# Two encoder layers on one core: three more couples of the down-projections by seven products, weight sums in place, split pieces through a ring of six

## The chip, the core and the metric

The kernel runs on one core of a Trainium2 chip. The core has a matrix engine (TensorE, PE in the profile; the loading of its stationary operand is listed as PEld), VectorE (DVE), ScalarE (ACT), GpSimd (POOL) and SyncE (SP), which here only issues DMAs, and 16 DMA engines that move data between HBM and the on-chip memory. Engines run their own instruction streams and wait for one another by semaphores. The metric is the device time of one execution in microseconds, as the median of several runs.

## The reference

What must be computed is a two-layer encoder trunk over 256 tokens of width 2048, in float32. Layer 0 mixes tokens by a bidirectional mLSTM, layer 1 by a bidirectional HGRN2. Each mixer and each feed-forward block has an RMSNorm ahead and a residual sum behind, and a last RMSNorm closes the trunk. The change is in the feed-forward blocks (and in what they share with the mixers' output projections):

```python
def conv_glu(hn, w_up, conv_w, conv_b, w_down):     # D_FF = 5504, CONV_W = 3
    u = hn @ w_up
    a, v = jnp.split(u, 2, axis=-1)
    s = a.shape[1]
    pad = CONV_W // 2
    ap = jnp.pad(a, ((0, 0), (pad, pad), (0, 0)))
    c = conv_b
    for j in range(CONV_W):
        c = c + ap[:, j:j + s] * conv_w[j]
    return (jax.nn.gelu(c, approximate=False) * v) @ w_down
...
for layer in range(DEPTH):
    hn = rmsnorm(h, norm_mix_g[layer])
    h = h + (mlstm_mixer if layer == 0 else hgrn_mixer)(hn, ...)
    h = h + conv_glu(rmsnorm(h, norm_ffn_g[layer]), ...)
return rmsnorm(h, final_g)
```

## The kernel before, in words

**Split products.** A float32 product is made of matmuls in a reduced format: each operand is a high part plus the rest, and high x high, high x rest and rest x high are summed. `parts` makes the two pieces of a weight: ScalarE copies a loaded tile to the high part `wh` (L137), VectorE subtracts it to get `wl` (L138). Both have four buffers of 1024 columns (`WB`). A weight tile arrives in one of three `raw` buffers by a DMA that SP issues.

**The stream.** All weight-heavy work is one list of chunks that `stream` runs through in order, with `split_weights` fetching pieces three ahead (`LOOK`). There are three kinds. An "fm" chunk holds 16 k-tiles and gives 256 features by 256 tokens with the weights stationary (L328 and L332). A "tm" chunk gives 256 tokens by 512 features with the activations stationary (L344). An "st" chunk, made by `pair`, gives two blocks of 512 output features at once by 2x2 squares of Strassen and Winograd: two k-tiles form a couple, in which the activations are A11, A12, A21, A22 (two token halves by two k-tiles) and the weights B11, B12, B21, B22. A plain couple takes eight products of three matmuls (128 x 512), a couple "by seven" takes seven of them, with four sums of activations (S1 to S4, `token_sums`) and four sums of weights (T1 to T4, `weight_sums`) in place of the plain operands. Products are accumulated in eight PSUM banks: four `mm` banks for P1, P5, P6 and P7 and four `aux` banks named `pc` for C11 to C22 (L237). After the last couple by seven, `mid` adds the four P banks to the residual `hm` in the on-chip memory (L546 to L554; the last two adds are on POOL), and after the last couple of the chunk `done` adds the four C banks (L559).

**A feed-forward block.** It has two parts, with 22 and 21 of the 43 blocks of 128 features. Part 0 is 22 fm chunks for the up-projection, then two pairs over the same 22 k-tiles, d0 and d1, 11 couples each. Part 1 is 21 fm chunks, one pair d0 of ten couples and a single k-tile, and then two tm chunks for the rest of the output, d2. Behind each fm chunk `done_up` scales by the norm's R, makes the convolution (a middle tap with the bias, then two shifted taps), Gelu, the product by v and the split of the result, which becomes the stationary operand of the pair. `SEVEN` says which couples go by seven: 7 of 11 in d0 of part 0, 6 in d1, and 6 in the pair of part 1, so 19 in each layer.

**Where weight sums come from.** For six couples of each pair (`STORED`) the sums are worked out beforehand: during the fm chunks `prepare` loads the four squares of a couple into four tiles (tags `th0`, `th1`, `tl0`, `tl1`), runs `weight_sums` on VectorE, and writes the sums to a scratch in HBM (`tscr`). In the pair, `combine` gets them back as two tiles `T` of 1024 columns and splits them into `th0`, `tl0`, `th1`, `tl1` (L209 and L210), each with one buffer. The seventh couple of d0 has its sums made on the spot. The outer projections of the mixers use the same code through `mixed`, with three couples by seven of eight (`SEVEN_MIX`), their sums made on the spot.

**What sets the order.** Each engine's instruction stream is put in order at build time by a scheduler that simulates the program; only instructions given to `pin` are kept where they are written. Extra work on the side (`prepare`, late norms) is a generator that `side.tick` advances as the matmuls are emitted. SP issues its DMAs in its own order, the loads for weights and for sums together with the stores of sums. TensorE's code itself is brought in by a DMA queue, listed in the profile as an instruction queue. In the HGRN mixer, which lies between the two feed-forward blocks, every head has a burst of many tiny float32 matmuls (`pd` and `pa`, L984), and the heads come in four groups.

Of the kernel before, what the change touches and what calls it, by code (L numbers as in the profile page):

```python
# [15 lines left out]
P = 128  # L16
# [27 lines left out]
WB = 4  # L44
MIX = 5
# [3 lines left out]
SEVEN = (1, 2, 4, 5, 7, 8, 9), (1, 2, 4, 5, 7, 8), (1, 2, 4, 5, 7, 8)  # L49
STORED = (1, 2, 4, 5, 7, 8)  # L50
# [10 lines left out]
def trunk_kernel(ctx, tc, xT, x_d, fg_d, pp_d, cst_d, w_gate, w_first, w_aq, w_ak, w_av, w_ao, w_aout, w_ao2,  # L61
# [63 lines left out]
    pin = tc.keep_in_program_order  # L125

# [5 lines left out]
    def split_weights(chunks):  # L132

        def parts(r, m, pin=lambda ins: ins):
            wh = wpool.tile([P, 1024], F32R, tag="wh", bufs=WB, name="wh")
            wl = wpool.tile([P, 1024], F32R, tag="wl", bufs=WB, name="wl")
            pin(act.copy(wh[:, :m], r))  # L137
            pin(dve.tensor_tensor(wl[:, :m], r, wh[:, :m].bitcast(F32), ALU.subtract))  # L138
            return wh, wl
# [33 lines left out]
    def temporary(pool_, name):  # L173
        return pool_.tile([P, 1024], F32, tag="avc", bufs=TEMP if pool_.name == "ff" else 2, name=name)

    def weight_sums(a, b, T, T_):

        B22, B21, B12 = a[:, 512:1024], b[:, 0:512], b[:, 512:1024]
        dve.tensor_tensor(T.rearrange("p (a b) -> p a b", a=2), B12.unsqueeze(1).broadcast_to([P, 2, 512]),
                          a.rearrange("p (a b) -> p a b", a=2), ALU.subtract)  # L180
        yield 2.5
        dve.tensor_tensor(T_[:, 0:512], B22, T[:, 0:512], ALU.subtract)
        yield 2.5
        dve.tensor_tensor(T_[:, 512:1024], B21, T_[:, 0:512], ALU.subtract)

    def split_squares(ch, parts):

        units, raws, kept, sums = (ch.nk + 1) // 2, {}, {}, {}
        side.until(lambda: ch.waits is None or ch.waits)

        def raw(u):
            if u not in raws and u < units:
                raws[u] = load_raw(ch.src, 2048 * u, min(2048 * (u + 1), 1024 * ch.nk) - (512 if u in ch.stored else 0))
                if u in ch.stored:
                    kept[u] = [temporary(ch.pool, "T") for _ in range(2)]
                    for t, src in zip(kept[u], ch.stored[u]):
                        nc.sync.dma_start(t, src)
            return raws.get(u)

        def combine(u):  # L200
            r = raw(u)
            T, T_ = kept[u] if u in kept else (temporary(ch.pool, "T") for _ in range(2))
            if u not in kept:
                for _ in weight_sums(r[:, 0:1024], r[:, 1024:2048], T, T_):
                    pass
            sums[u] = []
            for i, t in enumerate((T, T_)):
# [1080 lines left out]
```

## Time and profile before

| what | value |
|---|---|
| median of 3 runs | 2391.03 us (2389.68 to 2392.11) |
| span of the profiled execution | 2388.5 us, 2.5 us less than that median |
| TensorE busy | 2372.4 us, 99% of the span, at full clock |
| VectorE busy | 1944.1 us, 81% |
| ScalarE busy | 1298.8 us, 54% |
| POOL busy | 189.7 us, 8% |
| DMA | 555.07 MB, mean 232 GB/s |

The profile is one execution of the program, taken on the core; its times are microseconds from the start of the span. The page gives each engine's busy time, the chain of work that ended last (from the last instruction back, at each step to what released it), the costliest groups of instructions and the DMAs. A row of a group reads: line, engine, operation, output <- input by the program's names, shape and count, then busy time, mean nanoseconds of one, and the idle time just before them with what ended it. A row of a chain or a timeline reads: start, duration, engine, line, and what it is. A row of the windows reads: start and end, then the sum of the busy times of the engines in the order that the text gives, with numbers of instructions, then the granted clock, the DMA engines' busy share, and GB/s.

### The profile page before, as it was taken

The numbers are of one execution on the slowest core, as the hardware profiler recorded it, in microseconds if no ns is written. First come the engines' busy times: TensorE is split into PE (matmuls) and PEld (weight loads), VectorE is DVE, ScalarE is ACT, GpSimd is POOL, SyncE is SP. The second block draws the span as 40 slices with busy tenths as digits, with TensorE's granted clock in tenths as the row PEclk, the third lists the DMA queues.
The fourth block names the chain that finished last, engine by engine and source line by source line (L and its number), as shares of the span: only waits on it lengthen the run. The fifth ranks groups of instructions, "written<-read, shape, count | busy, mean of one in ns | idle before, by whom it ended". The sixth has DMA issues, their size and how long they took to land.

```text
span 2388.5 us, 37988 instructions
## 1 busy us (share of the span) xinstructions
PE 2372.4 (99%) x14614; PEld 2030.4 (85%) x14614; DVE 1944.1 (81%) x3221; ACT 1298.8 (54%) x2013; POOL 189.7 (8%) x240
## 2 busy tenths in 40 slices
PE   9999999999999999999999999999999999999998
PEld 7888888888888888888888888888888888888887
DVE  7766687988887888777888888888889888788874
ACT  7655455454564554555555555555555565454563
POOL 0100000000000000001222222220000000000000
PEclk9999999999999999999999999999999999999999
DMA  8654556988787777755554554545798888677774
GB/s 300 201 180 165 183 178 211 333 294 317 269 293 254 251 239 262 273 194 182 173 171 168 175 177 160 177 166 188 258 325 298 298 281 296 231 249 263 249 266 148
DMA packets 98789, 555.07 MB, mean 232 GB/s; under 512 B 11168, under 2 KB 11680, under 8 KB 50736
## 3 DMA queue, kind: packets, MB, share of 16 engines
q1 hardware_dynamic: 96912, 548.64, 65.6%
q0 software_dynamic: 1120, 3.21, 0.7%
q8 instruction: 114, 1.87, 0.3%
q10 hardware_dynamic: 576, 0.79, 0.1%
q14 instruction: 67, 0.55, 0.1%
HBM read 512.69 MB, written 39.91 MB: 231 GB/s over the span
## 4 chain that ended last, share of the span: by engine, by line
PE 98%; DVE 1%; issue 1%; DMA 0%; ACT 0%; SPq 0%; POOLq 0%; POOL 0%
PE mm L328 37%; PE mm L344 23%; PE mm L332 18%; PE pc L237 12%; PE mm L237 5%; PE pn L776 1%; PE py L1034 1%; PE pd L984 1%; PE pz L405 0%; PE pa L984 0%; DMA raw<-in_w_first 0%; PE S L762 0%; DVE tl L210 0%; PE pz L1055 0%; PE pa L1009 0%
## 5 line engine op out<-in xcount | busy, mean ns | idle before, releaser
L328 PE MATMUL mm<-xt,wh 128*128 128x512 f32 x3776 | 1313.4, 394 | 0.0
L137 ACT CAST wh<-raw 128x1024 fp32r<-128x1024 f32 (+1 forms) x846 | 853.5, 1019 | 693.8 <-PE mm L328 237.9
L138 DVE TENSOR_TENSOR wl<-raw,wh 128x1024 fp32r<-128x1024 f32 (+1 forms) x846 | 1004.7, 1195 | 265.1 <-ACT wh L137 257.6
L332 PE MATMUL mm<-xt,wl 128*128 128x256 f32 x3776 | 1045.9, 278 | 0.0
L328 PEld LDWEIGHTS mm<-xt,wh 128*128 128x128 f32 x3776 | 706.2, 188 | 159.4
L332 PEld LDWEIGHTS mm<-xt,wl 128*128 128x128 f32 x3776 | 709.5, 188 | 4.5 <-issue 0.4
L344 PE MATMUL mm<-wh,xt 128*128 128x512 f32 x1024 | 320.5, 391 | 3.0 <-ACT xt L350 1.3
L344 PEld LDWEIGHTS mm<-wh,xt 128*128 128x128 f32 x1024 | 191.4, 188 | 43.3 <-ACT xt L350 1.7
L344 PE MATMUL mm<-wl,xt 128*128 128x512 f32 x512 | 198.2, 391 | 0.0
L237 PE MATMUL pc<-wh,g 128*128 128x512 f32 x508 | 167.2, 389 | 0.0
L355 ACT COPY b<-mm 128x256 f32<-128x256 f32 x236 | 87.4, 370 | 122.9 <-PE mm L332 122.7
L210 DVE TENSOR_TENSOR tl<-T,th 128x1024 fp32r<-128x1024 f32 x88 | 109.9, 1264 | 38.9 <-ACT th L209 36.7
L209 ACT CAST th<-T 128x1024 fp32r<-128x1024 f32 x88 | 92.7, 1054 | 73.6 <-PE mm L237 43.5
L237 PEld LDWEIGHTS pc<-wh,g 128*128 128x128 f32 x508 | 95.4, 188 | 19.9
L344 PEld LDWEIGHTS mm<-wl,xt 128*128 128x128 f32 x512 | 96.2, 188 | 18.9
L553 POOL TENSOR_TENSOR hm<-hm,u 128x512 f32<-128x512 f32 x8 | 10.4, 1302 | 1150.9 <-DVE u L552 1150.9
L237 PE MATMUL pc<-wl,g 128*128 128x512 f32 x254 | 98.9, 389 | 0.0
L344 PE MATMUL mm<-wh,g 128*128 128x512 f32 x308 | 96.6, 392 | 0.0
L237 PE MATMUL mm<-th,sx 128*128 128x512 f32 x264 | 91.9, 390 | 0.0
L356 DVE TENSOR_TENSOR avc<-mm,b 128x256 f32<-128x256 f32 x172 | 72.0, 418 | 14.7 <-ACT b L355 14.7
L361 DVE TENSOR_TENSOR avc<-avc,R 128x256 f32<-128x256 f32 x172 | 71.9, 419 | 1.6
L976 DVE COPY kq<-QK 128x256 f32<-128x256 f32 x224 | 69.7, 336 | 0.0
(260 smaller groups left out, 2476.7 us busy)
## 6 DMA issues: line engine op xcount, KB each, us to landing
raw<-in_w_up SPq DMA_DIRECT2D x172, 1024.0 KB, 5.5
raw<-in_w_d SPq DMA_DIRECT2D x48, 1024.0 KB, 5.0
raw<-in_w_bq SPq DMA_DIRECT2D x48, 1024.0 KB, 4.9
pth<-in_w_d SPq DMA_DIRECT2D x72, 512.0 KB, 6.7
tscr<-ptl SPq DMA_DIRECT2D x72, 512.0 KB, 4.7
T<-tscr SPq DMA_DIRECT2D x72, 512.0 KB, 5.1
raw<-in_w_d SPq DMA_DIRECT2D x36, 768.0 KB, 5.2
raw<-in_w_ao SPq DMA_DIRECT2D x24, 1024.0 KB, 4.8
```

Source lines behind the costliest of these rows:

```text
L137: pin(act.copy(wh[:, :m], r))
L138: pin(dve.tensor_tensor(wl[:, :m], r, wh[:, :m].bitcast(F32), ALU.subtract))
L209: act.copy(th, t)
L210: dve.tensor_tensor(tl, t, th.bitcast(F32), ALU.subtract)
L237: pe.matmul(ps, a, b, start=id(ps) not in begun, stop=stop and i == 2)
L328: pe.matmul(ps[f], wh[:, c:c + P], x, start=k + kk == 0, stop=False)
L332: pe.matmul(ps[f][:, 0:T], wl[:, c:c + P], x[:, 0:T], start=False, stop=k + kk == ch.nk - 1)
L344: pe.matmul(ps[t], x[:, a + t * P:a + (t + 1) * P], w[:, c], start=st and i == 0, stop=sp and i == 2)
L355: act.copy(b, ps[:, T:2 * T])
L356: dve.tensor_tensor(dst, ps[:, 0:T], b, ALU.add)
L361: dve.tensor_tensor(dst, dst, R, ALU.mult)
L976: dve.tensor_copy(m[:, j].rearrange("k (m p j) -> k m p j", p=2, j=h), blocks(z, h, 0, T))
```

## The change

- `SEVEN` becomes 8 couples of 11 in both pairs of part 0 and 6 of 10 in part 1: 22 couples by seven in each layer. All of them have their sums stored, and `STORED` is gone. The scratch holds 2 x 8 + 6 sets of sums for each layer instead of 18.
- `prepare` loads a couple's four squares into two tiles of 1024, one couple ahead, computes the four sums in place with four subtractions of 512 columns, and stores both tiles. Their tags are `wh` and `wl` of the feed-forward pool, with two buffers each (`MORE`).
- In an st chunk the split pieces all go through `parts`. Every third one takes the feed-forward pool's two buffers, so that `wh` and `wl` have six in all. A couple by seven has four pieces, in the order B11 and B22, T2 and T3, B21 and T1, T4, and the matmuls follow it. Pieces are fetched three ahead, as before, and each of the four counts as one. T1 is loaded into the free last quarter of the `raw` tile, the rest of the sums into one tile `T` of 1536 columns. `th` and `tl` are gone.
- In `done_up` the conv's middle tap is made by ScalarE (an activation with scale and bias) instead of VectorE, and the two products by R become one of 512 columns. The bounce tile `b` is left out there.
- `token_sums` writes S4 to the unused half of the last-but-one activation tile or to a tile of its own.
- `banks` allocates the `mm` banks two at a time, by the same tag as before.

```diff
-SEVEN = (1, 2, 4, 5, 7, 8, 9), (1, 2, 4, 5, 7, 8), (1, 2, 4, 5, 7, 8)
-STORED = (1, 2, 4, 5, 7, 8)
+MORE = 2
+SEVEN = (1, 2, 3, 4, 6, 7, 8, 9), (1, 2, 4, 5, 7, 8)
...
-        def parts(r, m, pin=lambda ins: ins):
-            wh = wpool.tile([P, 1024], F32R, tag="wh", bufs=WB, name="wh")
-            wl = wpool.tile([P, 1024], F32R, tag="wl", bufs=WB, name="wl")
+        def parts(r, m, pin=lambda ins: ins, more=None):
+            where, bufs = wpool, WB
+            if more is not None:
+                turns["w"] += 1
+                if turns["w"] % 3 == 0:
+                    where, bufs = more, MORE
+            wh, wl = (where.tile([P, 1024], F32R, tag=n, bufs=bufs, name=n) for n in ("wh", "wl"))
             pin(act.copy(wh[:, :m], r))
             pin(dve.tensor_tensor(wl[:, :m], r, wh[:, :m].bitcast(F32), ALU.subtract))
             return wh, wl
...
         def raw(u):
             if u not in raws and u < units:
-                raws[u] = load_raw(ch.src, 2048 * u, min(2048 * (u + 1), 1024 * ch.nk) - (512 if u in ch.stored else 0))
+                n = 1536 if u in ch.stored else min(2048, 1024 * ch.nk - 2048 * u)
+                raws[u] = load_raw(ch.src, 2048 * u, 2048 * u + n)
                 if u in ch.stored:
-                    kept[u] = [temporary(ch.pool, "T") for _ in range(2)]
-                    for t, src in zip(kept[u], ch.stored[u]):
-                        nc.sync.dma_start(t, src)
+                    kept[u] = temporary(ch.pool, "T")
+                    nc.sync.dma_start(kept[u], ch.stored[u][:, 0:1536])
+                    nc.sync.dma_start(raws[u][:, 1536:2048], ch.stored[u][:, 1536:2048])
             return raws.get(u)
...
         for u in range(units):
             r = raw(u)
-            if u + 1 in ch.seven and not ch.late:
+            yield *parts(r[:, 0:1024], 1024, more=ch.pool), 1
+            if u + 1 in ch.seven and u + 1 not in ch.stored:
                 combine(u + 1)
...
+            if u in ch.seven:
+                yield *parts(kept[u][:, 0:1024], 1024, more=ch.pool), 1
             if 2 * u + 1 < ch.nk:
...
+                yield *parts(r[:, 1024:2048], 1024, more=ch.pool), 1
+            if u in ch.seven:
+                yield *parts(kept[u][:, 1024:1536], 512, more=ch.pool), 1
...
             if u in ch.seven:
...
+                S1, S3, S2, S4 = ch.sums(u)
+                products((P1, A11, B11), (C12, S4, B22))
+                T2, T3 = piece()
+                products((P6, S2, T2), (P7, S3, T3))
+                B21, T1 = piece()
+                products((C11, A12, B21), (P5, S1, T1))
+                T4, _ = piece()
+                products((C21, A22, T4))
...
     def prepare(mp, todo, period, finished):
...
+        yield 18.0
+        load(0)
+        for i, (_, dst) in enumerate(todo):
+            yield period / 2
+            load(i + 1)
+            B11, B22, B21, B12 = (loaded[i][j // 2][:, j % 2 * 512:(j % 2 + 1) * 512] for j in range(4))
+            for x, y, out in ((B12, B22, B22), (B12, B11, B12), (B11, B22, B11), (B21, B11, B21)):
+                dve.tensor_tensor(out, x, y, ALU.subtract)
+                yield period / 8
+            for j in range(2):
+                nc.sync.dma_start(dst[:, j * 1024:(j + 1) * 1024], loaded[i][j])
...
-                fm_scaled(ps[0], R, a)
-                fm_scaled(ps[1], R, v)
+                for z, p in ((a, ps[0]), (v, ps[1])):
+                    act.copy(z, p[:, T:2 * T])
+                    dve.tensor_tensor(z, p[:, 0:T], z, ALU.add)
+                av = avc[:, 0:2 * T].rearrange("p (a b) -> p a b", a=2)
+                dve.tensor_tensor(av, av, R.unsqueeze(1).broadcast_to([P, 2, T]), ALU.mult)
                 cw = [col("conv_w", (layer * 3 + w) * FT + f) for w in range(3)]
-                dve.tensor_scalar(c, a, cw[1], col("conv_b", layer * FT + f), ALU.mult, ALU.add)
+                act.activation(c, a, AF.Identity, bias=col("conv_b", layer * FT + f), scale=cw[1])
```

More of the change, by code (lines that the diff above doesn't have):

```diff
@@ L198, in raw @@
             return raws.get(u)
         def combine(u):
[L201 to L207, printed above, removed]
[L208 to L211 removed]
+            r, T = raw(u), temporary(ch.pool, "T")
@@ L594, in sums @@
             return SX[u]
-        two = pair(w2, KT, 1, x, sums, norm, SEVEN_MIX, True)
+        two = pair(w2, KT, 1, x, sums, norm, SEVEN_MIX)
         def token():
@@ L1152, in two @@
                 return ch
-            chunks.append(two(w_d0[layer][:, f0 * 1024:(f0 + nf) * 1024], 0, nxt if part else None, SEVEN[2 * part]))
+            chunks.append(two(w_d0[layer][:, f0 * 1024:(f0 + nf) * 1024], 0, nxt if part else None, SEVEN[part]))
             if part:
@@ L1159, in ffn @@
             else:
-                chunks.append(two(w_d1[layer], 2, None, SEVEN[1]))
+                chunks.append(two(w_d1[layer], 2, None, SEVEN[0]))
         return chunks, stack.close
```

128 lines of the change are left out of this document (62 added, 66 removed).

## The prediction, made before the result was known

> **What bounds the kernel now.** I read the page first, then the waits of TensorE, then a table by stage.
>
> ```profile
> span 2388.5 us, 37988 instructions
> PE 2372.4 (99%) x14614; PEld 2030.4 (85%) x14614; DVE 1944.1 (81%) x3221; ACT 1298.8 (54%) x2013; POOL 189.7 (8%) x240
> ...
> PE 98%; DVE 1%; issue 1%; DMA 0%; ACT 0%; SPq 0%; POOLq 0%; POOL 0%
> ```
>
> TensorE is busy all the time and is 98% of the chain that ends last. So time goes only with TensorE's own instructions or with its few waits, and it comes only from a new wait of TensorE. These are its waits (in all, times, longest):
>
> ```profile
> PE pd L984 <- issue: 2.6, 2, 1.4
> ...
> PE mm L344 <- issue: 0.9, 1, 0.9
> PE mm L344 <- ACT wh L137: 0.8, 1, 0.8
> PE mm L237 <- DVE tl L210: 0.6, 2, 0.3
> ```
>
> In layer 0 the stages that the change touches are the first up-projections (22 chunks), the pair d0, the pair d1, the other 21 up-projections, and the last pair. The columns are busy time of PE, PEld, DVE, ACT, POOL, then clock, DMA share and GB/s:
>
> ```profile
> 389.70:635.30 245.60, 245.60 (x1421) 214.78 (x1420) 215.77 (x363) 128.45 (x192) 0.70 (x1) 1.00 0.82 295
> 635.30:690.40 55.10, 55.10 (x245) 45.63 (x244) 44.20 (x51) 33.88 (x40) 0.00 (x0) 1.00 0.84 296
> 690.40:747.00 56.60, 56.30 (x248) 46.09 (x247) 46.99 (x48) 31.56 (x35) 7.09 (x4) 1.00 0.74 262
> 747.00:979.90 232.90, 232.90 (x1344) 203.64 (x1344) 194.01 (x317) 117.81 (x174) 0.00 (x0) 1.00 0.73 250
> ```
>
> Full clock, no gap in PE but 0.3 us, VectorE and the DMA engines at four fifths: this is what a new wait has to come from.
>
> **The change part by part.** *Three more couples by seven products in each layer (19 to 22).* A product is three matmuls of 128x512, so 6 couples take away 18 matmuls. The chain shows a whole plain couple:
>
> ```profile
> 1027.79 5.44 PE pc L237 x24
> ```
>
> 5.44 / 24 = 0.2267 us each; 18 x 0.2267 = 4.1 us less. Nothing lies beside TensorE, so all of it counts: **-4.1 us**.
>
> *TensorE's code moves.* Waits put down to "issue" stand in three of the four groups of heads of the HGRN layer, always at the end of a head's burst of tiny matmuls. The chain has them:
>
> ```profile
> 1206.43 0.70 PE pd L984 x41
> 1207.13 1.24 issue
> 1208.37 0.26 PE pd L984 x5
> ```
>
> ```profile
> 1330.86 0.71 PE pd L984 x42
> 1331.56 1.38 issue
> ```
>
> ```profile
> 1455.39 0.73 PE pd L984 x43
> 1456.13 0.66 PE mm L344 x2
> 1456.79 0.87 issue
> ```
>
> And the fourth group, as a window, has none (PE 1.60 of 1.60):
>
> ```profile
> 1579.00:1580.60 1.60, 1.60 (x130) 1.56 (x130) 1.57 (x4) 1.48 (x5) 0.00 (x0) 1.00 0.04 10
> ```
>
> The code comes by a queue of its own:
>
> ```profile
> q8 instruction: 114, 1.87, 0.3%
> ```
>
> 29228 records of PE and PEld in 114 packets are 256 instructions a packet. A head's burst (line 984) is 64 float32 matmuls of four instructions each: one block, gone in 1.3 us. If a block's edge lies at the start of the burst, the next edge lies at its end, before the next block can be there. I counted TensorE's instructions in the built order (two for a split matmul or a transpose, four for a plain float32 one, one for a wait). All three stalls are at the same place, count 195 modulo 256, and the four bursts begin 9 after, 2 after, 5 before and 12 before that edge. So the position decides: 1.24, 1.38, 0.87 and 0 us. In the changed kernel everything from here on lies 16 earlier (9 matmuls less in layer 0, two waits more). The four bursts then begin 7, 14, 21 and 28 before the edge; in the other twelve the edge lies 62 to 216 instructions inside, as now (46 to 200). Between 5 and 12 before, 0.87 falls to 0, so 7 before gives about 0.6. The waits' 2.6 + 0.9 = 3.5 us become 0.6: **-2.9 us**; the ends are -3.5 (all gone) and 0 (as many as now). I take the first reading, since one position fits all four rows.
>
> [...]
>
> *Splits through a ring of six; the sums' own single buffers go.* TensorE's 0.6 us behind `tl` arose when d1 follows d0. There POOL adds to hm, and a VectorE instruction stands still beside it:
>
> ```profile
> 693.31 0.68 DVE L552 TENSOR_TENSOR u<-u,mm 128x512 f32<-128x512 f32 x1
> 693.90 0.68 DVE L559 TENSOR_TENSOR hm<-hm,pc 128x512 f32<-128x512 f32 x1
> 694.50 4.27 DVE L210 TENSOR_TENSOR tl<-T,th 128x1024 fp32r<-128x1024 f32 x2
> ```
>
> ```profile
> 695.41 2.29 POOL L554 TENSOR_TENSOR hm<-hm,u 128x512 f32<-128x512 f32 x1
> ```
>
> ```profile
> 682.40 2.35 DVE L138 TENSOR_TENSOR wl<-raw,wh 128x1024 fp32r<-128x1024 f32 x2
> ...
> 684.67 2.35 DVE L210 TENSOR_TENSOR tl<-T,th 128x1024 fp32r<-128x1024 f32 x2
> ```
>
> The same two splits take 4.27 instead of 2.35 us: 1.9 us lost. With six pieces ahead instead of a single `tl` this loss is covered there: **-0.6 us** (ends -0.6 and 0). But the built order of layer 0 puts VectorE's work so: after P5 is complete four adds of mid, two splits for d1, and only then the add that frees the bank of C11, which d1's first matmul needs. By the starts above an add takes 0.6 us and a split 1.14: 4 x 0.6 + 2 x 1.14 + 0.6 = 5.3, and 7.2 with POOL's 1.9. TensorE has 27 matmuls left, 6.1 us. So a new wait of **+1.1 us** (0 if POOL falls elsewhere). In layer 1 the built order has the bank's add ahead of POOL's work: 0.
>
> *VectorE and ScalarE in the up stages.* These are the durations:
>
> ```profile
> L138 DVE TENSOR_TENSOR wl<-raw,wh 128x1024 fp32r<-128x1024 f32 x782 | 963.8, 1237 | 257.0 <-ACT wh L137 249.6
> L210 DVE TENSOR_TENSOR tl<-T,th 128x1024 fp32r<-128x1024 f32 x88 | 109.9, 1264 | 38.9 <-ACT th L209 36.7
> L361 DVE TENSOR_TENSOR avc<-avc,R 128x256 f32<-128x256 f32 x172 | 71.9, 419 | 1.6
> L179 DVE TENSOR_TENSOR ptl<-pth 128x1024 f32<-128x1024 f32 x36 | 44.0, 1223 | 26.5 <-DMA pth<-in_w_d 22.7 <-issue 3.6
> L138 DVE TENSOR_TENSOR wl<-raw,wh 128x512 fp32r<-128x512 f32 x64 | 43.9, 686 | 8.1 <-ACT wh L137 8.1
> L1118 DVE TENSOR_SCALAR avc<-avc,pp 128x256 f32<-128x256 f32 x86 | 34.9, 406 | 0.0
> L532 DVE TENSOR_TENSOR avc<-avc 128x128 f32<-128x128 f32 x104 | 30.0, 288 | 2.0
> L182 DVE TENSOR_TENSOR ptl<-pth,ptl 128x512 f32<-128x512 f32 x36 | 24.6, 683 | 0.0
> ```
>
> In the first up stage the middle tap leaves VectorE (22 x 0.41 = -8.9), two multiplications by R become one of 512 (22 x (2 x 0.42 - 0.68) = -3.5), 16 preparations of 4 x 0.68 stand for 12 of 1.22 + 2 x 0.68 (+12.6), and token sums are 8 instead of 7 with one instruction more (+3). That is +3 on 215.8 of 245.6 us: hidden, 27 us of room. ScalarE gets 22 taps of about the Gelu's length, +9 on 128. If VectorE waited for each tap, the room allows 1.2 us a chunk before TensorE is touched. The other up stage loses VectorE work.
>
> In a pair, a couple by seven costs VectorE 3 x 1.24 + 0.69 = 4.4 us (before 1.24 + 0.69 + 2 x 1.26 = 4.45) in TensorE's 21 x 0.2267 = 4.76: it fits, with 0.36 us to spare, but now in runs of four couples (1 to 4, 6 to 9). No cost taken; the cover is the six pieces, and if it goes a run costs about one split, 1.1 us.
>
> *DMA.* A couple with stored sums brings the same bytes as before, cut otherwise (768 KB, 768 KB and 256 KB against these):
>
> ```profile
> T<-tscr SPq DMA_DIRECT2D x72, 512.0 KB, 5.1
> raw<-in_w_d SPq DMA_DIRECT2D x36, 768.0 KB, 5.2
> ```
>
> 768 + 2 x 512 KB = 1.835 MB in 4.76 us are 385 GB/s through a run of four; over d0 it is 328 against 296, in the first up stage 326 against 295 (16 preparations of 2 MB for 12). SP issues them in order, so sums wait behind the last preparation's stores, with three raw buffers ahead. What the engines carry when they are pressed:
>
> ```profile
> 485.00:492.00 7.00, 7.00 (x43) 6.13 (x42) 3.28 (x5) 3.66 (x6) 0.00 (x0) 1.00 1.02 426
> ```
>
> Full at about 420 GB/s, so 385 passes and I cost it at 0.
>
> **Sum.** -4.1 - 2.9 - 0.6 + 1.1 = -6.5 us. The profiled span of 2388.5 us becomes 2382.0; 2.5 us lie between the span and the median of the runs, 2391.03, so 2384.5 us, -0.27%. A measurement of this kernel tells about 0.2% (4.8 us) from no change.
>
> **The rivals.** *The DMA engines don't carry a run of four (slower).* For it: the stage row says 296 GB/s at a share of 0.84, so 352 when full. Then a couple takes 1.835 MB / 352 = 5.21 us, 0.45 late; 32 such couples make 14.4 us, and -6.5 + 14.4 is 2398.9 us. It decides from 0.35 us a couple on (11.3 us), that is at under 359 GB/s and with nothing loaded ahead. Against it: 426 GB/s for 7 us.
>
> [...]
>
> *The code's waits stay (no difference).* If the blocks' arrival is not tied to the count but to what the DMA engines do then, 3.5 us stay: -3.6, 2387.4 us. For it: the stalls are 124 us apart, as the groups are. Against: the fourth group.
>
> *VectorE is late in the runs of four (no difference).* Eight runs of four at 0.5 us each are 4 us: -2.5, 2388.5 us. For: 0.36 us to spare and one hop more by ScalarE per chunk; against: six pieces ahead.
>
> That the change doesn't do what it says is excluded for the products: the built order has 18 matmuls fewer.
>
> **How the numbers follow.** The sum as worked out, or a little better, 0.60, by itself 2381.5 to 2386; the code's waits or VectorE, 0.24; the DMA engines 0.16. The range goes from the best ends (-4.1 - 3.5 - 0.6 = -8.2, 2382.8, less the runs' 1.3) to half of the DMA rival's loss: 2381 to 2393. Faster 0.60, same 0.24, slower 0.16.
>
> **What would show it.** Matmuls of 128x512 18 fewer; waits for "issue" under 1 us in all; no wait for `wl` but one of about a microsecond where d1 begins in layer 0, for VectorE. The first up stage of 245 us with VectorE at some 219 and the DMA share near 0.9. Wrong would be: TensorE waiting for `wh` or `wl` inside couples 1 to 4 or 6 to 9, with ScalarE waiting for T or raw (DMA) or VectorE without a gap (its rival); or "issue" of 3 us again.

## The result, and the profile after

The changed kernel takes 2394.91 us (median of 21 runs, 2388.76 to 2398.15) beside 2390.35 us (2388.69 to 2394.18) for the kernel before: a ratio of 1.0017, with a 95% interval of 1.0010 to 1.0023. I had forecast 2384.5 us and a faster kernel. It is not faster, it is slower by 4 us or so, and its times spread twice as far.

The profiled execution is one of the quickest (span 2388.1 us), so one of ordinary length is read beside it (span 2392.4 us; the run "again" below). The page of the first, its busy times and the chain that ended last:

```profile
PE 2371.3 (99%) x14596; PEld 2027.1 (85%) x14596; DVE 1939.6 (81%) x3167; ACT 1352.4 (57%) x2141; POOL 189.7 (8%) x240
...
PE 90%; DMA 6%; DVE 3%; issue 1%; ACT 0%; SPq 0%; POOLq 0%; POOL 0%; DVEq 0%; ACTq 0%
```

The 18 matmuls are gone (14614 to 14596 in the records). But the chain that was 98% TensorE now runs for 9% of the span through DMAs and VectorE. TensorE's waits, in the same execution (in all, times, longest):

```profile
PE mm L229 <- ACT wh L142: 2.8, 2, 1.5
...
PE mm L334 <- DVE wl L143: 1.1, 2, 0.9
...
PE mm L346 <- issue: 0.3, 1, 0.3
```

and in the ordinary one:

```profile
PE mm L334 <- DVE wl L143: 3.6, 7, 1.0
PE mm L229 <- ACT wh L142: 3.3, 2, 2.1
...
PE mm L346 <- issue: 0.4, 1, 0.4
```

The waits for the code ("issue") fell from 3.5 to 0.3 and 0.4 us. The new ones are for split pieces: in the up-projections (L334, where there was none) and in the pairs (L229). By stage, in the ordinary execution (columns as before; the rows are the first up stage and d0 of layer 0, then of layer 1):

```profile
388.90:638.40 249.50, 247.41 (x1421) 215.38 (x1420) 211.59 (x352) 135.52 (x216) 0.70 (x1) 1.00 0.88 315
638.40:696.00 57.60, 54.69 (x238) 43.94 (x237) 49.32 (x59) 39.03 (x49) 1.67 (x1) 1.00 0.97 365
...
1679.60:1927.60 248.00, 246.45 (x1421) 215.35 (x1420) 211.48 (x351) 133.84 (x214) 0.70 (x1) 1.00 0.89 316
1927.60:1984.00 56.40, 54.29 (x233) 42.89 (x233) 48.59 (x58) 40.53 (x52) 0.00 (x0) 1.00 0.96 365
```

The up stages took 245.6 and 245.7 us before and take 249.5 and 248.0 us; d0, 55.1 us before in both layers with more matmuls, takes 57.6 and 56.4. VectorE has less to do in the up stage than before (211.6 against 215.8 us), and the granted clock is 1.00. Where the time comes from is seen in the chain that ended last of the first execution, between 590 and 655 us. Each row is a start, a length, and what it is:

```profile
592.01 9.87 DMA pwl<-in_w_d
...
602.00 0.69 DVE pwl L598
...
605.99 7.21 DMA tscr<-pwl
...
613.22 7.55 DMA pwl<-in_w_d
...
621.77 0.86 DVE wl L143
...
623.87 6.92 DMA tscr<-pwh
...
630.89 2.01 ACT wh L142 x2
...
632.92 1.23 DVE wl L143
...
634.60 8.52 DMA T<-tscr
...
646.09 5.46 DMA T<-tscr
...
651.58 1.05 ACT wh L142
```

`pwh` and `pwl` are the preparations' tiles, L598 their subtraction. A preparation's load takes 7 to 10 us here (6.8 to 9.9 us from issue to landing for `pwl`); VectorE stands before its first subtraction until it has landed, and the split `wl` behind it is late. The store of a preparation's sums must land before the tiles are loaded again. The store of the last preparation but one (623.87) ends 6 us before the pair begins, at 630.79. Only then does ScalarE split the next weights (630.89), because two of the ring's six buffers are the preparations' tiles. The pair's first sums `T` are issued behind that split's `wl` and behind the last preparation's stores. The next sums (646.09) go out when VectorE is done with the split of the first and with the last up chunks' tile `avc`, which shares three buffers with `T`.

VectorE's waits for the preparations' loads, before and after:

```profile
DVE ptl L179 <- DMA pth<-in_w_d: 22.7, 16, 3.9
```

```profile
DVE pwl L598 <- DMA pwl<-in_w_d: 27.9, 15, 4.1
DVE pwh L598 <- DMA pwh<-in_w_d: 21.6, 13, 3.0
```

They doubled. The experiments ask which of this costs TensorE its time.

### The profile page after: what moved, and what is told of

The parts are those of the page before. It is cut to its first block, busy times and chain, and to the rows that moved or that the text cites. A ratio compares the mean times of both kernels' runs of the same rounds, so it can differ in the third digit from the quotient of the medians.

```text
span 2388.1 us, 38126 instructions
## 1 busy us (share of the span) xinstructions
PE 2371.3 (99%) x14596; PEld 2027.1 (85%) x14596; DVE 1939.6 (81%) x3167; ACT 1352.4 (57%) x2141; POOL 189.7 (8%) x240
## 4 chain that ended last, share of the span: by engine, by line
PE 90%; DMA 6%; DVE 3%; issue 1%; ACT 0%; SPq 0%; POOLq 0%; POOL 0%; DVEq 0%; ACTq 0%
PE mm L330 32%; PE mm L346 23%; PE mm L334 16%; PE pc L229 10%; PE mm L229 5%; DMA pwl<-in_w_d 2%; DVE wl L143 1%; DMA T<-tscr 1%; DMA pwh<-in_w_d 1%; PE pn L793 1%; PE py L1051 1%; DMA tscr<-pwl 1%; PE pd L1001 0%; PE pz L407 0%; PE pa L1001 0%
## 5 line engine op out<-in xcount | busy, mean ns | idle before, releaser
L143 DVE TENSOR_TENSOR wl<-raw,wh 128x1024 fp32r<-128x1024 f32 (+1 forms) x846 | 1033.4, 1227 | 268.7 <-ACT wh L142 265.3
L142 ACT CAST wh<-raw 128x1024 fp32r<-128x1024 f32 (+1 forms) x846 | 874.4, 1040 | 567.1 <-PE mm L330 265.6
L334 PE MATMUL mm<-xt,wl 128*128 128x256 f32 x3776 | 1046.6, 278 | 1.1 <-DVE wl L143 1.1
L334 PEld LDWEIGHTS mm<-xt,wl 128*128 128x128 f32 x3776 | 709.5, 188 | 6.5 <-DVE wl L143 2.0
L229 PE MATMUL pc<-wh,g 128*128 128x512 f32 x576 | 195.1, 390 | 0.3 <-ACT wh L142 0.2
L229 PEld LDWEIGHTS pc<-wh,g 128*128 128x128 f32 x576 | 108.0, 188 | 24.8 <-ACT wh L142 2.0
L229 PE MATMUL pc<-wl,g 128*128 128x512 f32 x288 | 112.3, 390 | 0.9 <-DVE wl L143 0.9
L143 DVE TENSOR_TENSOR wl<-T,wh 128x1024 fp32r<-128x1024 f32 (+1 forms) x100 | 93.8, 951 | 21.7 <-ACT wh L142 21.3
L229 PE MATMUL mm<-wh,sx 128*128 128x512 f32 x300 | 107.1, 391 | 2.8 <-ACT wh L142 2.8
L142 ACT CAST wh<-T 128x1024 fp32r<-128x1024 f32 (+1 forms) x100 | 82.3, 835 | 45.7 <-PE pc L229 23.3
L1138 ACT ACTIVATE avc<-avc,pp 128x256 f32<-128x256 f32 x86 | 51.6, 600 | 87.7 <-DVE avc L1136 87.7
L1133 ACT COPY avc<-mm 128x256 f32<-128x256 f32 x172 | 63.7, 371 | 51.4 <-PE mm L334 50.9
L598 DVE TENSOR_TENSOR pwl<-pwl 128x512 f32<-128x512 f32 x88 | 60.2, 684 | 27.9 <-DMA pwl<-in_w_d 27.9
L598 DVE TENSOR_TENSOR pwh<-pwh 128x512 f32<-128x512 f32 x88 | 60.2, 684 | 27.8 <-DMA pwh<-in_w_d 21.6
```

The lines of the kernel that those rows point to most:

```text
L229: pe.matmul(ps, a, b, start=id(ps) not in begun, stop=stop and i == 2)
L334: pe.matmul(ps[f][:, 0:T], wl[:, c:c + P], x[:, 0:T], start=False, stop=k + kk == ch.nk - 1)
L598: dve.tensor_tensor(out, x, y, ALU.subtract)
L1133: act.copy(z, p[:, T:2 * T])
L1138: act.activation(c, a, AF.Identity, bias=col("conv_b", layer * FT + f), scale=cw[1])
```

## The experiments

Theory A says that the bytes for the sums in the pairs are too many for the DMA engines (my slower rival). Theory B says that VectorE, the ring or the split pieces are late by their own work. Theories C and E were formed on the way: C is stated below at the run seven, and E says that the preparations end too near the pair.

### The code's position, and the changed kernel again

"again" is the changed kernel without an edit; its lines are shown above.

> The changed kernel once more, to see an execution of its ordinary length (2395 us; the profiled one was 2390). If the DMA engines bind the pair d0 (theory A), the 5 us more lie where that execution already waits: behind sums and their splits in the last microseconds of the first up stage and in d0 of both layers, 6.5 us of TensorE's waits there becoming 10 to 13, with the DMA share at 0.95 or more. If instead VectorE or the ring is late by its own work (theory B), the waits lie anywhere in the runs of four couples with VectorE busy without a gap and the DMA share below 0.9. If the difference is outside the changed stages, neither.

Measured: 2394.93 us, ratio 1.0024 (1.0013 to 1.0034). The 5 us more lie in the up stages (3.6 instead of 1.1 us of waits there, now in both layers) as much as in d0. Theory A had them in the last microseconds of the up stage and in d0 alone; theory B in the runs of four alone. Neither reads right.

"code" is the kernel before with another count of warm-up matmuls:

```diff
-    for i in range(90):
+    for i in range(86):
```

> The kernel before with 86 instead of 90 warm-up matmuls at the start, which moves all of TensorE's later code 16 instructions up, to the position that the HGRN layer has in the changed kernel; nothing else. If the position in blocks of 256 sets the waits for issue behind the bursts of tiny matmuls, their 3.5 us fall to 0.3 (what the changed kernel shows) and the time falls by 3.2 us to 2387.2. If they come from what the DMA engines do at that time, 3.5 us stay and the time is the same.

Measured: 2386.28 us, ratio 0.9985 (0.9976 to 0.9994) beside 2389.66 us: 3.4 us less. Of the waits for "issue" one is left:

```profile
PE mm L344 <- issue: 0.2, 1, 0.2
```

So the position alone makes these waits, as counted in the prediction.

### The number of couples

"seven": one couple less by seven in each pair of part 0, the rest of the change kept.

```diff
-SEVEN = (1, 2, 3, 4, 6, 7, 8, 9), (1, 2, 4, 5, 7, 8)
+SEVEN = (1, 2, 4, 5, 7, 8, 9), (1, 2, 4, 5, 7, 8)
...
-    for i in range(90):
+    for i in range(87):
```

> The changed kernel with one couple less by seven in each pair of part 0 (7, 7 and 6 of them; runs of two, two and three couples), and 87 warm-up matmuls, so that the HGRN layer's code lies as in the changed kernel. All else of the change stays: sums in place, ring of six, middle tap on ScalarE. Against the kernel before it has 6 matmuls less (-1.4 us) and the code's waits (-3.2 us). Theory A (bytes for sums in long runs): d0 needs about 310 GB/s, no waits, -4.6 us, 2385.8. Theory B (ring, splits, in-place sums or the tap cost time by themselves): the waits stay, 2390 or more.

Measured: 2416.7 us, ratio 1.0116 (1.0102 to 1.0130). Fewer bytes and fewer preparations, and 27 us slower than before. TensorE's waits:

```profile
PE mm L334 <- DVE wl L143: 15.5, 15, 1.8
PE mm L229 <- ACT wh L142: 4.8, 4, 2.5
```

They are in the up stages, where theory A has nothing to say. VectorE's timeline at one of them (start, length, and in brackets how long it was idle before and for what) has this row:

```profile
503.55 0.69 DVE L598 TENSOR_TENSOR pwh<-pwh 128x512 f32<-128x512 f32 x1 [5.02 <-DMA pwh<-in_w_d]
```

VectorE stands five microseconds before a preparation's load, with the splits queued behind it. Theory C: this standing is the cause.

"fly" keeps all 22 couples, but makes the sums of couples 1 and 6 on the spot.

```diff
+FLY = 1, 6
...
                 for u in seven:
+                    if seven is SEVEN[0] and u in FLY:
+                        continue
                     ch.stored[u] = tscr[box["n"]]
```

> The changed kernel with couples 1 and 6 of both pairs of part 0 by sums made on VectorE on the spot, not stored: 12 preparations instead of 16 in the first up stage, and two sets of sums less to load in each pair; the products are those of the changed kernel (18 matmuls less than before). Theory A: d0 falls from 365 to about 305 GB/s, the DMA share to some 0.85, the waits of 6.5 us and more go: -4.1 - 3.2 = -7.3 us, 2383. Theory B: VectorE has 5.5 us more to do in d0 and the waits grow: 2396 or more.

Measured: 2388.92 us, ratio 0.9997 (0.9989 to 1.0006). The up stages are clean (no wait of L335, this kernel's number for the up-projection's second matmul), and the waits stand in the pairs:

```profile
PE mm L230 <- ACT wh L143: 2.1, 3, 1.2
PE mm L230 <- DVE wl L144: 1.6, 3, 1.0
```

Twelve preparations leave the up stage alone, and VectorE's extra sums come due in the pairs instead. Between 2383 and 2396 this decides nothing about A.

### Without preparations, and without loads for sums

"noprep" has no preparations; the pairs load their sums' bytes from the weights.

```diff
-                    ch.stored[u] = tscr[box["n"]]
+                    ch.stored[u] = src[:, 2048 * u:2048 * (u + 1)]
...
-                side.push(prepare(box["mp"], todo, (nf * 10.4 - 26.0) / len(todo), finished))
+                finished.append(True)
```

> The changed kernel without any preparation: no loads, subtractions or stores for sums in the up stages; the pairs load as many bytes from the weights in place of the sums, so those couples' products are not the reference's. Theory C: TensorE waits neither in the up stages nor at the start of the pairs (stages of 245.7 and 109.7 us), 2382 to 2383. Theory A: 245.7, but the pair still 112.6 us, at 365 GB/s with the DMA share above 0.95.

"nosums" keeps the preparations and loads no sums in the pairs.

```diff
-                n = 1536 if u in ch.stored else min(2048, 1024 * ch.nk - 2048 * u)
+                n = min(2048, 1024 * ch.nk - 2048 * u)
...
-                    kept[u] = temporary(ch.pool, "T")
-                    nc.sync.dma_start(kept[u], ch.stored[u][:, 0:1536])
-                    nc.sync.dma_start(raws[u][:, 1536:2048], ch.stored[u][:, 1536:2048])
+                    kept[u] = raws[u]
```

> The changed kernel, but in the pairs the sums' pieces are made from the couple's own weights: nothing is loaded for sums there (1 MB for a couple instead of 1.75), and those couples' products are not the reference's. Preparations stay. Theory C: the up stages keep their 2 to 4 us of waits in layer 0; the pairs lose only what hung on late sums. Theory A: the pairs are clean (109.7 us) and the up stages keep theirs.

Measured, in one run each: noprep 2380.59 us, nosums 2391.52 us, beside 2391.25 us. The first up stage and d0 of noprep, and a run of four couples in d0:

```profile
389.80:635.40 245.60, 245.60 (x1421) 214.78 (x1420) 189.88 (x297) 138.72 (x220) 0.70 (x1) 1.00 0.59 195
635.40:689.50 54.10, 54.10 (x241) 44.80 (x240) 43.98 (x50) 36.46 (x44) 0.00 (x0) 1.00 0.89 337
...
665.40:684.50 19.10, 19.10 (x86) 15.83 (x85) 16.00 (x17) 14.79 (x17) 0.00 (x0) 1.00 0.90 332
```

TensorE is busy for every microsecond of both, in couples whose bytes are those of the changed kernel. Theory A falls: the pair by itself is carried. So does theory B for the ring, the tap and the split pieces, which are all in this kernel (here no preparation holds two of the ring's buffers). In nosums the up stages keep their waits (3.8 us for `wl`), as both theories had it. The 14 us between the changed kernel's 2394.9 and noprep's 2380.6 go with the preparations. And d0 still waits in nosums, without a load for sums: one wait, where the pair of layer 1 begins, is this.

```profile
PE pc L227 <- ACT wh L142: 2.8, 1, 2.8
```

### Moving the subtractions

"pin" keeps a preparation's subtractions in program order on VectorE, so that they come later than the loads; "sevenpin" is the same in seven.

```diff
-                dve.tensor_tensor(out, x, y, ALU.subtract)
+                pin(dve.tensor_tensor(out, x, y, ALU.subtract))
```

> The changed kernel, with the four subtractions of a preparation kept in program order on VectorE (behind all that was written before them), so that they come half a period or more behind their loads and not right where the scheduler takes the loads as landed; 88 warm-up matmuls keep the HGRN layer's code where it lies in the changed kernel. If VectorE standing before a preparation's loads is the cause (theory C; 2 to 4 us each in the run called again), its waits for these loads fall from 53 to under 10 us, TensorE's waits in the first up stages (2.2 and 4.0 us in layer 0, 0 and 2.4 us in layer 1) go, and those at the start of the pair shrink because the last feature chunks end earlier: 2386 to 2388. If the bytes in the pair are the cause (theory A), the up stages are clean and the pair's 3 us in each layer stay: 2390.

> The run called seven (7, 7 and 6 couples) with the same subtractions kept in program order, 86 warm-up matmuls. Theory C: the stalls each 18 us in the up stages (10.7 and 15 us of TensorE's waits) go, and with two preparations fewer the pairs are clean too: -1.4 - 3.2 = 2385.5. If something else makes VectorE late, 2405 or more stays.

"behind1" and "behind4" hold only the first subtraction, behind the last split written before it.

```diff
+            load(i)
+            yield BEHIND
...
+            with tc.issue_after(turns["wl"]):
+                dve.tensor_tensor(B22, B12, B22, ALU.subtract)
```

> The changed kernel with only the first subtraction of each preparation kept behind one instruction of VectorE, the last split written before it, which is written 1.5 ticks after the couple's loads (in the changed kernel the scheduler puts it about 8 us behind their issue); the loads of a couple are written half a period later than before. 88 warm-up matmuls keep the code's position. Theory C: the first subtraction comes 11 us or more behind the loads, VectorE's waits for them (53 us in the run called again) fall below 15, TensorE's waits in the first up stages go and those at the start of the pairs shrink: 2384 to 2387. If VectorE's standing is not the cause but the last preparation ending 7 us before the pair (theory E), the up stages get clean and the pairs keep 2 to 3 us each: 2387 to 2390.

> The same with 4 ticks between the loads and the instruction that the first subtraction stands behind; 87 warm-up matmuls. Theory C: VectorE's waits for loads near zero, the time as in behind1 or lower by up to 1 us; theory E: the preparations end 2.5 us later, the pairs wait longer, slower than behind1 by 1 to 3 us.

"pool" has the subtractions on POOL.

```diff
-                dve.tensor_tensor(out, x, y, ALU.subtract)
+                pool.tensor_tensor(out, x, y, ALU.subtract)
```

> The changed kernel with the preparations' subtractions on POOL instead of VectorE (1.3 us each by POOL's adds of this size in the kernel before). Theory C: VectorE waits for no preparation's loads; POOL may. VectorE loses 0.9 us beside each (from the 1.9 us that two of POOL's adds cost before), 16 x 4 x 0.9 = 58 us for 44 us saved in an up stage, so it is at some 226 of 245.6 us and TensorE's waits in the up stages fall below 2 us each. If VectorE's share decides and not the standing still, they grow.

Measured: pin 2494.61 (ratio 1.0432), sevenpin 2424.70 (1.0138), behind1 2481.85 (1.0381), behind4 2549.31 (1.0667), and pool, in one run, 2398.47 us. All misses. VectorE hardly stands before loads any more (17.7 us in behind4, at most 0.5 us in the others), and other waits came in their place. In behind1, SyncE's own waits are these:

```profile
SPq L603 <- DVE pwl L601: 109.0, 28, 12.6
SPq L603 <- DVE pwh L601: 108.6, 40, 10.9
```

SyncE stands before the stores of the sums (L603), and the weights' loads are behind them in its order. So these five changed the lateness of one queue into that of another. They don't test theory C; they show that a preparation's chain (load, subtract, store) is threaded through two queues that TensorE's weights use too.

### Which part of a preparation

"copy" loads and stores as before and subtracts nothing.

```diff
-            for x, y, out in ((B12, B22, B22), (B12, B11, B12), (B11, B22, B11), (B21, B11, B21)):
-                dve.tensor_tensor(out, x, y, ALU.subtract)
-                yield period / 8
+            yield period / 2
```

> The changed kernel with preparations that load and store the weights themselves, without the four subtractions, so the couples by seven of the feed-forward blocks are not the reference's; bytes and DMAs are those of the changed kernel. If VectorE's standing before the loads is the cause (theory C), TensorE's waits in the first up stages and in the pairs go and it takes about 2381 to 2383. If the bytes and SyncE's order are, they stay: 2388 to 2395.

"still" subtracts, without further loads and stores.

```diff
+            if 1 < i < len(todo):
+                loaded.append(loaded[i % 2])
-            if i < len(todo):
+            elif i < len(todo):
...
-            for j in range(2):
-                nc.sync.dma_start(dst[:, j * 1024:(j + 1) * 1024], loaded[i][j])
```

> The changed kernel with the subtractions of all preparations on tiles that are loaded once per stage, without further loads and without stores (the pairs load as many bytes from the weights; those products are not the reference's); 87 warm-up matmuls for the code's position. Theories C and bytes: no waits, 2381 to 2382. If VectorE's work itself is too much (44 us in a stage), the waits stay.

"early" ends the preparations sooner.

```diff
-                side.push(prepare(box["mp"], todo, (nf * 10.4 - 26.0) / len(todo), finished))
+                side.push(prepare(box["mp"], todo, (nf * 10.4 - 44.0) / len(todo), finished))
```

> The changed kernel with preparations 1.1 ticks closer to each other, so that the last one is written 18 ticks (19 us) earlier. If the end of the preparations just before the pair is the cause (theory E), the waits at the end of the up stage and in the pair go and the time is 2384 to 2386. Theory C: the loads press each other more, VectorE stands longer, and the waits move into the up stage: 2393 or more.

"fly6" is fly with couple 6 alone, and 14 preparations at the pace of 16.

```diff
+FLY = 6,
...
-                side.push(prepare(box["mp"], todo, (nf * 10.4 - 26.0) / len(todo), finished))
+                side.push(prepare(box["mp"], todo, (nf * 10.4 - 26.0) / (16 if nf == FA else 6), finished))
```

> The changed kernel with couple 6 of both pairs of part 0 by sums made on the spot (it follows a plain couple, in which VectorE has 2.9 us free), and the remaining 14 preparations at the pace of the 16, so that they end two periods earlier. Products as in the changed kernel. By the run called again, where the waits before the 14th preparation were 1.3 us in layer 0 and 0.8 us in layer 1: up stages nearly clean, pairs with some 1 us each (VectorE): 2390 - 7.3 + 2.1 + 2 = 2387. If a late end is no cause, the waits of 6 us in the pairs stay: 2391.

Measured: copy 2382.06 us and still 2402.41 us, in one run each, early 2386.09 us (ratio 0.9984, 0.9975 to 0.9994), fly6 2383.85 us (0.9970, 0.9961 to 0.9980), beside 2390.40 us.

The first up stage and d0 of copy:

```profile
391.50:637.10 245.60, 245.60 (x1421) 214.88 (x1420) 190.20 (x297) 138.51 (x220) 0.70 (x1) 1.00 0.93 331
637.10:691.20 54.10, 54.10 (x241) 44.79 (x240) 43.98 (x50) 36.68 (x44) 0.00 (x0) 1.00 0.88 340
```

All the loads and stores are there, the DMA engines are at a share of 0.93 in the up stage (0.88 in again), and TensorE waits nowhere. So the bytes are not the cause in the up stage either, nor the stores' place in SyncE's order by itself. It takes the subtractions in VectorE's order. Their work alone is no cause, since VectorE has less to do in this stage than in the kernel before (211.6 against 215.8 us).

still didn't test what it was for. With nothing to wait for, the scheduler put all 64 subtractions of a stage into its first 115 us, and TensorE waited there for VectorE (12.8 us for `avc`). It tells one thing: after these, the rest of the up stage and the pairs (109.0 us, as in copy) are clean.

early and fly6 bear out theory E in the main. TensorE's longest waits for pieces in all of early:

```profile
PE mm L334 <- DVE wl L143: 1.0, 2, 0.5
PE pc L229 <- ACT wh L142: 1.0, 2, 0.8
```

and in all of fly6:

```profile
PE mm L335 <- DVE wl L144: 0.9, 2, 0.6
PE mm L230 <- DVE wl L144: 0.9, 1, 0.9
```

What ties the end of the preparations to the pair is seen in SyncE's issues (start, time to issue, what): the last stores of sums and the first sums loaded, in the kernel before, where the pair begins at 635 us, and in the changed one, where it begins at 637 us.

```profile
601.90 0.33 SPq L583 DMA_DIRECT2D tscr<-ptl  x1
621.65 3.32 SPq L197 DMA_DIRECT2D T<-tscr  x2
```

```profile
623.87 3.27 SPq L601 DMA_DIRECT2D tscr<-pwh  x2
629.86 2.14 SPq L601 DMA_DIRECT2D tscr<-pwl  x2
634.60 0.42 SPq L192 DMA_DIRECT2D T<-tscr  x1
```

The last stores of sums went out 20 us ahead of the first `T` before, and 5 us ahead of it after. In all the traces in which the first sums loaded are those of couple 1 and VectorE's order was left to the scheduler, the time from the first `T`'s issue to the pair's first product into a C bank goes with TensorE's waits in d0 (the excess of matmul starts over 0.227 us, those over 0.09 us summed):

| kernel | layer 0: ahead, waits (us) | layer 1: ahead, waits (us) |
|---|---|---|
| before | 13.8, 0 | 13.8, 0 |
| code | 13.0, 0 | 12.6, 0 |
| copy | 13.2, 0 | 13.2, 0 |
| noprep | 10.7, 0 | 13.1, 0 |
| still | 10.8, 0 | 13.5, 0 |
| fly6e | 11.1, 0 | 13.5, 0 |
| fly6 | 7.9, 0.6 | 13.2, 0 |
| sevenpace | 8.6, 0.8 | 10.7, 0 |
| pool | 4.4, 3.5 | 6.7, 1.4 |
| early | 3.4, 2.4 | 9.4, 0 |
| after | 2.6, 3.2 | 0.7, 3.5 |
| again | 2.3, 4.0 | 0.7, 3.5 |
| early2 | 2.3, 6.0 | 7.2, 2.4 |
| seven | 3.1, 6.8 | 3.1, 1.9 |

From 9.4 us ahead on there is no wait, from 8.6 us down there always is one. So the loss in d0 goes with first sums that are issued late, at the end of preparations that come too near the pair. By which way is not settled. By the same measure nosums, which loads no sums, still waits 0.9 and 3.1 us in d0, so late sums are not all of it. And in layer 0 of early the last stores went out 8 us sooner than in the changed kernel (621.7), but the first sums only at 633.4: SyncE issues them behind a weight load that waits for a `raw` buffer, that is for VectorE's splits. The gain of early is in layer 1. No run gave the preparations or `T` buffers of their own.

### The pace of the preparations

"sevenpace" is seven at the pace of the changed kernel:

```diff
-                side.push(prepare(box["mp"], todo, (nf * 10.4 - 26.0) / len(todo), finished))
+                side.push(prepare(box["mp"], todo, (nf * 10.4 - 26.0) / (16 if nf == FA else 6), finished))
```

> The run called seven with its 14 preparations at the pace of the changed kernel (12.7 ticks instead of 14.5), so that they end two periods earlier; nothing else. If the pace, by where each load's landing falls in the work of a feature chunk and how near the pair the last one ends, makes the 27 us, the up stages show below 2 us of waits each and the pairs below 2: 2385 to 2388. If the couples' pattern or their number makes it, 2410 or more stays.

"early2" begins the preparations 10 ticks earlier (`yield 8.0` for `yield 18.0`, and 34.0 for 26.0 in the pace); "fly6e" does the first in fly6.

> The changed kernel with all 16 preparations, the first written 10 ticks earlier and the pace at 12.2 ticks, so that the last is written 18 ticks earlier than in the changed kernel, as in the run called early (11.6 ticks). Pairs as clean as there; up stages with fewer waits if a slower pace lets the loads land earlier: 2384 to 2386.

> The run called fly6 with its 14 preparations written 10 ticks earlier at the same pace. The waits in the up stage of layer 0 (1.3 us) may move; the pair's first wait goes; the wait of 1.1 us where d1 begins stays: 2383.

Measured: sevenpace, in one run, 2388.81 us beside 2389.75; early2 2397.26 us, ratio 1.0026 (1.0013 to 1.0039); fly6e 2389.87 us, 0.9999 (0.9989 to 1.0009).

sevenpace shows that seven's loss was its pace, 14.5 ticks instead of 12.7 (a tick is the unit of the side work's clock, about 1 us): the waits of 15.5 us in the up stages are gone. VectorE's standing fell less, by these rows from 62.7 us to 48.0 (seven, then sevenpace):

```profile
DVE pwh L598 <- DMA pwh<-in_w_d: 32.7, 11, 5.0
DVE pwl L598 <- DMA pwl<-in_w_d: 30.0, 12, 4.5
```

```profile
DVE pwh L598 <- DMA pwh<-in_w_d: 24.1, 13, 3.4
DVE pwl L598 <- DMA pwl<-in_w_d: 23.9, 16, 3.1
```

So theory C holds only in part. It takes VectorE's standing (copy has none, and no wait), but its sum says little: 48 us cost TensorE next to nothing here, 51 us cost it 0.9 us in the up stages of fly6, and 53 us cost 3.6 us in again. What sets the price of a stand was not shown. Starting earlier (early2) made the up stage worse: VectorE's longest stand is 5.6 us there, and TensorE's one wait for a `wl` 2.6.

early2, fly6e and one stage of sevenpace lost in another way too: TensorE went through their first up stages at a longer pace, without a wait (the last section).

The quickest that computes the reference is fly6, 0.30% under the kernel before, with the 18 matmuls less and the code's position of the changed kernel. The run code, the kernel before with one number changed, gets half of that.

## Why the prediction was right or wrong

**18 matmuls, -4.1 us: right.** The two pairs of part 0 take 109.03 us together in copy, with nothing waiting, and 111.77 before: 2.7 us less for nine matmuls (2.0) and the wait for `tl` (0.5). Two layers make 5.5 us, for which I had 4.1 and 0.6.

**The code's waits, -2.9 us: right.** Measured 3.1 us less in the changed kernel's trace, and 3.4 us in the run that moved the code alone. What is left stands where the count put it, behind the burst of the first group.

**The wait for `tl`, -0.6 us: right**, there is none. **The new wait where d1 begins, +1.1 us: too dear.** In both traces of the changed kernel TensorE waits 0.26 us there in layer 0. The size isn't fixed: fly6 waits 0.9 us at the same place, for a `wl` (its row above).

**"+3 on 215.8 of 245.6 us: hidden, 27 us of room": the first step that failed.** VectorE's work even fell, to 211.6 us. But I took room as a sum over the stage. VectorE ran in order, and a subtraction whose load landed 2 to 4 us late held up the splits behind it. At the row of seven above, VectorE stands 5.02 us; the split behind its subtraction runs only at 505.15, though its `wh` was there (ScalarE had been idle for 6.15 us until 504.73), and TensorE waits 1.09 us for it. The room after that stand doesn't help a piece that TensorE needs now. The trace of before had the row of 22.7 us of such waits, and I had not asked what four preparations more in each layer would make of it: 53 us in the ordinary execution, with 3.6 us of TensorE's waits in two up stages that grew by 6 us.

**"385 passes and I cost it at 0": the second, for another reason than its own.** The rate does pass: the pairs of noprep and copy have no wait at the same bytes, and the engines moved 332 GB/s during a run of four, not 385. What failed is the sentence before it, that sums wait behind the last preparation's stores "with three raw buffers ahead". I named this queue and gave it no price. The last preparation's stores moved from 20 us to 5 us ahead of the first sums, and the first sums from 13.8 us to 2.6 and 0.7 us ahead of the pair, where the table has no wait from 9.4 us on: 3.2 and 3.5 us of waits in d0. The ring of six, which I took as six pieces ahead, also has two buffers that the preparations hold until their stores have landed.

The sum: of the 7.5 us gained in the profiled execution (4.1 + 3.1 + 0.6, less 0.3 at d1) all but 0.4 were given back (2388.5 to 2388.1); an ordinary one gives back 5 us more.

**The rivals.** The slower one had the right sign and a price of the right order (2398.9), by the wrong mechanism: the engines carry the runs of four (noprep and copy, no wait in d0). Its price came from 352 GB/s as all that they move. The changed kernel moved more than that through the middle of d0, with TensorE busy throughout:

```profile
670.00:675.00 5.00, 5.00 (x24) 4.14 (x23) 3.78 (x4) 3.92 (x5) 0.00 (x0) 1.00 1.02 414
675.00:680.00 5.00, 5.00 (x24) 4.14 (x23) 3.67 (x5) 3.70 (x5) 0.00 (x0) 1.00 1.02 418
```

That the code's waits stay was wrong. That VectorE is late in the runs of four by its own work was wrong too; it is late ahead of them. The sign named for the DMA rival did come, a wait for `wh` in couple 2 with ScalarE waiting for `T` (651.58), but from a late issue and not from the engines' rate. And the range's upper end, 2393, was set by halving the one loss I could price; a second mechanism of the same kind was not in it.

## What to carry to other kernels

Room on an engine that takes its work in order, as VectorE did here (5.02 us of standing in seven, with a split behind it that could have run), is not an average: for work put on the side, ask what instruction stands at the head of the queue when a transfer is late, and which piece is behind it. Where side work has a deadline, price its last item and not its mean: what is queued behind its last store, how far ahead of its use that must be issued (here 9.4 us were enough and 8.6 were not), and whose buffers it holds until then. This kernel's code came in 114 packets, and four warm-up matmuls less (the run code) took 3.4 us off: a kernel with waits for "issue" behind bursts of tiny matmuls is worth one try with a few instructions more or less at the start.

## What the runs showed of the hardware

**The same stream of matmuls ran at two steady paces.** In the up stage fly6e does some 2% fewer matmuls in a time than fly6, at full clock and without a wait in either window (the same stretch of fly6, then of fly6e):

```profile
410.00:560.00 150.00, 150.00 (x867) 131.15 (x866) 128.72 (x209) 81.48 (x128) 0.00 (x0) 1.00 0.91 323
```

```profile
410.00:560.00 150.00, 150.00 (x851) 130.17 (x850) 125.81 (x205) 80.80 (x126) 0.00 (x0) 1.00 0.88 311
```

Starts are 231, 112, 233, 117 ns apart in the first and 236, 113, 233, 117, 241, 120 ns in the second, for the whole stage. In the run pool the starts go from the first pattern to the second at a wait of 0.8 us, at 503 us. In fly6e and early2 TensorE has one wait instruction more, at 410.5 and 409.4 us in layer 0. Whether either is the cause was not tried, and one stage of sevenpace has the longer pace without it. It costs 4.4 us a stage, in both layers of fly6e, which has no waits for pieces at all and yet is no quicker than before.

**Behind two long waits TensorE's granted clock was 0.64 and 0.73 for some microseconds.** They are a wait of 2.5 us in seven and one of 2.6 us in early2; in the mean over the run the clock is 0.997 in both, and 0.999 in the kernel before:

```profile
663.00:668.00 5.00, 5.00 (x15) 3.92 (x15) 4.67 (x5) 3.52 (x4) 0.00 (x0) 0.64 0.70 216
```

```profile
553.70:560.00 6.30, 5.85 (x25) 5.07 (x26) 6.27 (x11) 3.29 (x7) 0.00 (x0) 0.73 0.77 259
```

The matmuls there start 427 ns apart instead of 227 or 230. In seven the first of these rows has 15 matmuls, and the next 5 us, at a clock of 1.00, have 23. Not every such wait does it: behind the 2.8 us in nosums the granted clock stayed at 1.00 (0.999 in the mean over that run), and what decides it was not shown. The wait in seven cost more than itself: the eleven matmuls behind it lost another 2 us.
